# A streaming logsumexp: heads shared anew between GpSimd and VectorE, summed one tile later, in stages

## The chip, the cores and the metric

The kernel runs on one core of one Trainium2 chip. The metric is device time in microseconds (us) of one execution. Engines: PE or TensorE multiplies matrices, DVE is VectorE, ACT is ScalarE, POOL is GpSimd, SP is SyncE, which here only issues transfers.

## The reference

For each of 8 batches, 2048 rows and 8 heads of 256 columns, add the head's bias, take the logsumexp over the 256 columns, and write each result twice in a row:

```
x_heads = x.reshape(B, S, H, Dh).transpose(0, 2, 1, 3) + bias[None, :, None, :]
x_tiled = np.repeat(x_heads, 2, axis=2)
mx = x_tiled.max(axis=-1, keepdims=True)
lse = mx.squeeze(-1) + np.log(np.exp(x_tiled - mx).sum(axis=-1))
```

The input is 134 MB of float32, the output 1 MB. The kernel leaves out the maximum: it sums exp(x + b), or exp(x) times exp(b), and takes the logarithm.

## The kernel before

The rows are cut into T = 64 tiles of 256 rows (8 a batch); a tile is 128 partitions x K = 2 rows x 2048 columns, 2 MB. Nine buffers `xts` hold tiles. The order on every engine is the order in the code (a manual schedule). SP issues the loads (L95): nine at the start, and at the end of step t the load of tile t - 1 + 9 (L322), once the buffer's last reader is done. The last two tiles are loaded in pieces (`LAST_CUTS`, L26): tile 62 in two halves (one row of each partition), tile 63 in two and five pieces.

Each tile's eight heads take one of three ways, all with exp on ScalarE:

- Heads 0 and 1: TensorE adds the bias into PSUM (`add_bias`, L154 and L159: a small matmul with the bias, split into three bf16 parts, then the tile through the identity). ScalarE takes exp of each head and sums it in the same instruction (`sum_biased`, L165), four instructions a tile.
- Heads 2 to 4: GpSimd adds the bias in place (`g_add`, L182, b_rep is the bias spread over the partitions). One step later ScalarE takes exp of all six (three heads, two rows, `exp_inplace`, L194) and VectorE sums them in one reduce (`g_sum`, L186).
- Heads 5 to 7: ScalarE takes exp of x alone (L194), and VectorE multiplies each head and row by exp(bias) and sums it in one instruction (`weigh`, L200), six a tile. exp(bias) lies in PSUM, in w_rep.

So a step t issues on ScalarE: exp of heads 5 to 7 of tile t, exp of heads 2 to 4 of tile t - 1, four sums of tile t; on VectorE: six weighs of tile t, one reduce of tile t - 1. The last two tiles have no GpSimd part (NLATE): ScalarE takes exp of heads 2 to 7 piece by piece, VectorE weighs all six.

The sums of a batch go to R. Two steps after a batch ends, `finish` (L211) transposes R on TensorE (L216), takes Ln on ScalarE (L229), and issues the store (L250), on SP in the bulk. At the end tile 62 has its own sums Ry, tile 63 Rz; their stores are on SP, and eight stores of the last batch's other tiles on GpSimd's queue.

Of the kernel before, what the change touches and what calls it, by code (L numbers as in the profile page):

```python
# [9 lines left out]
F32 = mybir.dt.float32  # L10
BF16 = mybir.dt.bfloat16
ACT = mybir.ActivationFunctionType
ALU = mybir.AluOpType


K = 2

NPE = 2
NG = 3
NLATE = 2
NBUF = 9

LAST_CUTS = [[0, 1024, 2048], [0, 512, 1024, 1536, 1792, 2048]]  # L26


@with_exitstack
def kernel(  # L30
# [6 lines left out]
    nc = tc.nc  # L37
    P = nc.NUM_PARTITIONS
    B, S, D = x.shape
    H, Dh = bias.shape  # L40
    assert D == H * Dh and S % (P * K) == 0
    NBLK = S // (P * K)
    T = B * NBLK
    CPE = NPE * Dh
    CW = D - CPE
    MM = 512
    assert CPE <= MM

    sb = ctx.enter_context(tc.tile_pool(name="sb", bufs=1))
    pp = ctx.enter_context(  # L50
        tc.tile_pool(name="pp", bufs=1, space=bass.MemoryType.PSUM)
    )

    brow = sb.tile([1, D], F32, name="brow")
    b_rep = sb.tile([P, NG * Dh], F32, name="b_rep")
    ident = sb.tile([P, P], F32, name="ident")
    ones = sb.tile([1, P], F32, name="ones")
    ones3 = sb.tile([3, P], BF16, name="ones3")
    b3 = sb.tile([3, CPE], BF16, name="b3")
    bparts = sb.tile([1, 3, CPE], BF16, name="bparts")  # L60
    brest = sb.tile([1, 2, CPE], F32, name="brest")

    nblk = [NBLK] * (B - 1) + [NBLK - 2]
    R = [sb.tile([P, K, H, nblk[b]], F32, name=f"R{b}") for b in range(B)]
    Ry = sb.tile([P, K, H], F32, name="Ry")
    Rz = sb.tile([P, K, H], F32, name="Rz")
    junk = [sb.tile([P, Dh], F32, name=f"junk{i}") for i in range(2)]
    res = [sb.tile([H * NBLK, P, K, 2], F32, name=f"res{i}") for i in range(2)]
    xts = [sb.tile([P, K, D], F32, name=f"xt{i}") for i in range(NBUF)]
    w_rep = pp.tile([P, CW], F32, name="w_rep")  # L70
    ps = [pp.tile([P, MM], F32, name=f"ps{i}") for i in range(4)]
    tpair = pp.tile([P, 2, K, P], F32, name="tpair")
    tps = [tpair[:, i] for i in range(2)]

    def pieces(t):

        left = T - 1 - t
        if left > 1:
            return [(0, K, 0, D)]
        cuts = [[0, D]] * K if left else LAST_CUTS  # L80
        return [
            (k, k + 1, c0, c1) for k in range(K) for c0, c1 in zip(cuts[k], cuts[k][1:])
        ]

    def rows_of(t):

        b, blk = divmod(t, NBLK)
        v = x[b, blk * P * K : (blk + 1) * P * K, :]
        if t < T - 1:
            return v.rearrange("(p k) d -> p k d", k=K)  # L90
        return v.rearrange("(k p) d -> p k d", k=K)

    def load(t):
        for k0, k1, c0, c1 in pieces(t):
            nc.sync.dma_start(  # L95
                out=xts[t % NBUF][:, k0:k1, c0:c1], in_=rows_of(t)[:, k0:k1, c0:c1]
            )
# [5 lines left out]
    for set_idx, (_name, funcs) in enumerate(get_activation_tables(nc.m.arch).items()):  # L103
        if ACT.Exp in funcs and ACT.Ln in funcs:
            nc.scalar.add_instruction(  # L105
                mybir.InstLoadActFuncSet(
                    name=nc.get_next_instruction_name(),
# [4 lines left out]
    nc.scalar.dma_start(out=brow, in_=bias.rearrange("h j -> (h j)").unsqueeze(0))  # L112
    for t in range(NBUF):
        load(t)
# [4 lines left out]

    bp = brow[:, 0:CPE]  # L120
    nc.gpsimd.tensor_copy(bparts[:, 0], bp)
# [5 lines left out]
        nc.gpsimd.dma_start(out=b3[i : i + 1, :], in_=bparts[:, i])  # L127

    for c in range(0, CW, MM):
        nc.tensor.matmul(  # L132
            w_rep[:, c : c + MM],
            lhsT=ones,
            rhs=brow[:, CPE + c : CPE + c + MM],
            start=True,
            stop=True,
        )
    nc.scalar.activation(out=b_rep, in_=w_rep[:, 0 : NG * Dh], func=ACT.Copy)  # L139
    for c in range(0, CW, MM):  # L140
        w = w_rep[:, c : c + MM]
        nc.scalar.activation(out=w, in_=w, func=ACT.Exp)  # L142


    n_ps = [0]
    n_junk = [0]

    def add_bias(views):

        got = []  # L150
        for v in views:
            p = ps[n_ps[0] % len(ps)]
            n_ps[0] += 1
            nc.tensor.matmul(  # L154
                p[:, 0:CPE], lhsT=ones3, rhs=b3, start=True, stop=False
            )
            got.append(p)
        for p, v in zip(got, views):
            nc.tensor.matmul(p[:, 0:CPE], lhsT=ident, rhs=v, start=False, stop=True)  # L159
        return got  # L160

    def sum_biased(p, dst):
        for h in range(NPE):
            c = h * Dh
            nc.scalar.activation(  # L165
                out=p[:, c : c + Dh],
                in_=p[:, c : c + Dh],
                func=ACT.Exp,
                accum_out=dst(h),
            )  # L170

    b_tile = bass.AP(
        tensor=b_rep.tensor,
        offset=b_rep.offset,
        ap=[b_rep.ap[0], [0, K], [1, NG * Dh]],
    )

    def g_part(t):
        return xts[t % NBUF][:, :, CPE : CPE + NG * Dh]

    def g_add(t):
        nc.gpsimd.tensor_tensor(out=g_part(t), in0=g_part(t), in1=b_tile, op=ALU.add)  # L182

    def g_sum(t):
        b, blk = divmod(t, NBLK)
        nc.vector.tensor_reduce(  # L186
            out=R[b][:, :, NPE : NPE + NG, blk],
            in_=g_part(t).rearrange("p k (h j) -> p k h j", j=Dh),
            op=ALU.add,
            axis=mybir.AxisListType.X,  # L190
        )

    def exp_inplace(v):
        nc.scalar.activation(out=v, in_=v, func=ACT.Exp)  # L194

    def weigh(v, h, dst):
        c = h * Dh - CPE
        j = junk[n_junk[0] % 2]
        n_junk[0] += 1
        nc.vector.tensor_tensor_reduce(  # L200
            out=j,
            in0=v,
            in1=w_rep[:, c : c + Dh],
            scale=1.0,
            scalar=0.0,
            op0=ALU.mult,
            op1=ALU.add,
            accum_out=dst,
        )
# [45 lines left out]
    def finish_batch(b, engine):  # L255
# [7 lines left out]
            engine,  # L263
        )

    for t in range(T):
        b, blk = divmod(t, NBLK)
        xt = xts[t % NBUF]
        left = T - 1 - t

        def sum_at(k, h):
            if left > 1:
                return R[b][:, k, h, blk : blk + 1]
            return (Ry if left else Rz)[:, k, h : h + 1]

        if left >= NLATE:

            got = add_bias([xt[:, k, 0:CPE] for k in range(K)])
            g_add(t)
            w0 = CPE + NG * Dh  # L280
            exp_inplace(xt[:, :, w0:D])
            if t:
                exp_inplace(g_part(t - 1))
            for k in range(K):
                sum_biased(got[k], lambda h: sum_at(k, h))
            for k in range(K):
                for c in range(w0, D, Dh):
                    weigh(xt[:, k, c : c + Dh], c // Dh, sum_at(k, c // Dh))
            if t:
                g_sum(t - 1)  # L290
        for k0, k1, c0, c1 in pieces(t) if left < NLATE else []:
            if left == 0 and c1 == D and k0 > 0:

                finish(
                    B - 1,
                    lambda k: Rz[:, k0 - 1],
                    1,
                    1,
                    S - (K - k0 + 1) * P,
                    0,  # L300
                    nc.sync,
                )
            if c0 == 0:
                got = add_bias([xt[:, k, 0:CPE] for k in range(k0, k1)])
            w0 = max(c0, CPE)
            if w0 < c1:
                exp_inplace(xt[:, k0:k1, w0:c1])
            if c0 == 0:
                for k in range(k0, k1):
                    sum_biased(got[k - k0], lambda h: sum_at(k, h))  # L310
            for k in range(k0, k1):
                for c in range(w0, c1, Dh):
                    weigh(xt[:, k, c : c + Dh], c // Dh, sum_at(k, c // Dh))
            if left == 0 and c0 == 0:
                if k0 == 0:
                    finish_batch(B - 1, nc.gpsimd)
                elif k0 == 1:
                    finish(B - 1, lambda k: Ry[:, k], 1, K, S - 2 * K * P, 0, nc.sync)
        if left == NLATE:
            exp_inplace(g_part(t))  # L320
            g_sum(t)
        if 0 < t and t - 1 + NBUF < T:  # L322
            load(t - 1 + NBUF)

        fb, at = divmod(t - 2, NBLK)
        if fb >= 0 and at == NBLK - 1:
            finish_batch(fb, nc.sync)
# [33 lines left out]
```

The softmax here doesn't subtract the row's maximum and nothing guards it: scores larger than these inputs give would overflow.

## Time and profile before

| what | value |
|---|---|
| median of 9 runs | 337.96 us (337.76 to 338.32) |
| the profiled execution's own time | 338.13 us |
| its span, first to last instruction | 336.4 us |
| busy: ScalarE, VectorE, TensorE, GpSimd | 301.4, 244.7, 233.8, 224.3 us |
| mean granted TensorE clock | 0.787 |
| transfers | 135.46 MB, mean 403 GB/s |
| instructions | 2806 |

How to read it: in the profile a group of instructions is one line: code line, engine, operation, output <- input, shapes, count, then busy time, mean ns of one, and the idle time of the engine just before them with what ended it. The slices cut the span into 40 equal parts of 8.41 us: a digit is the busy share in tenths. A line of the time-ordered list has start and length in us; two of a kind in a row can be one line. In the tables of stretches the columns are the stretch, its length, busy time of PE, PE's weight load, DVE, ACT and POOL (with the number of instructions), the granted TensorE clock, the share of the 16 DMA engines that is busy, and GB/s. In the last microseconds SP's last store runs; no other engine does.

### The profile page before, as it was taken

The numbers are of one execution on the slowest core, as the hardware profiler recorded it, in microseconds if no ns is written. First come the engines' busy times: TensorE is split into PE (matmuls) and PEld (weight loads), VectorE is DVE, ScalarE is ACT, GpSimd is POOL, SyncE is SP. The second block draws the span as 40 slices with busy tenths as digits, with TensorE's granted clock in tenths as the row PEclk, the third lists the DMA queues.
The fourth block names the chain that finished last, engine by engine and source line by source line (L and its number), as shares of the span: only waits on it lengthen the run. The fifth ranks groups of instructions, "written<-read, shape, count | busy, mean of one in ns | idle before, by whom it ended". The sixth has DMA issues, their size and how long they took to land.

```text
span 336.4 us, 2806 instructions
## 1 busy us (share of the span) xinstructions
PE 233.8 (70%) x410; PEld 68.7 (20%) x410; DVE 244.7 (73%) x856; ACT 301.4 (90%) x660; POOL 224.3 (67%) x84
## 2 busy tenths in 40 slices
PE   6297687756779477766676786595675866883961
PEld 2122222121122122221121121121121221121210
DVE  0248888798878768777868777777877777877784
ACT  1489999999999989999989999899998999998995
POOL 7866766766766766776666776666775776675704
PEclk9997877789765976789877758767877589578596
DMA  8999999999999999999999999999999999999910
GB/s 299 431 431 433 423 431 425 431 427 426 429 428 427 429 430 427 431 422 430 430 424 429 429 425 433 427 427 431 429 430 425 428 429 427 429 429 420 352 41 16
DMA packets 11204, 135.46 MB, mean 403 GB/s; under 512 B 1577, under 2 KB 1849, under 8 KB 2993
## 3 DMA queue, kind: packets, MB, share of 16 engines
q1 hardware_dynamic: 10832, 135.17, 95.1%
q0 software_dynamic: 352, 0.10, 0.2%
q14 instruction: 15, 0.12, 0.1%
q8 instruction: 3, 0.05, 0.1%
q10 hardware_dynamic: 2, 0.01, 0.0%
HBM read 134.23 MB, written 1.05 MB: 402 GB/s over the span
## 4 chain that ended last, share of the span: by engine, by line
DMA 71%; DVE 6%; ACT 5%; issue 1%; PE 0%; SPq 0%; ACTq 0%; DVEq 0%
DMA xt<-in_x_dram 71%; ACT xt L194 4%; DVE junk L200 3%; DVE R L186 2%; ACT ps L165 1%; ACT res L229 0%; PE ps L159 0%; PE tpair L216 0%; DVE Rz L200 0%; DVE R L200 0%; SPq L95 0%; ACTq L194 0%; DVEq L356 0%
## 5 line engine op out<-in xcount | busy, mean ns | idle before, releaser
L182 POOL TENSOR_TENSOR xt<-xt,b_rep 128x1536 f32<-128x1536 f32 x62 | 214.0, 3451 | 96.2 <-DMA xt<-in_x_dram 91.9
L159 PE MATMUL ps<-xt,ident 128*128 128x512 f32 x256 | 180.6, 843 | 76.0 <-DMA xt<-in_x_dram 75.4
L200 DVE CUSTOM_DVE_ANT_0 junk<-xt,w_rep 128x256 f32<-128x256 f32 x396 | 140.5, 418 | 86.6 <-ACT xt L194 86.6
L194 ACT ACTIVATE xt<-xt 128x1536 f32<-128x1536 f32 (+1 forms) x132 | 183.4, 1436 | 14.0 <-DMA xt<-in_x_dram 13.2
L186 DVE TENSOR_REDUCE R<-xt 128x6 f32<-128x1536 f32 x62 | 108.5, 1750 | 0.8 <-ACT xt L194 0.8
L165 ACT ACTIVATE ps<-ps 128x256 f32<-128x256 f32 x256 | 94.5, 369 | 10.1 <-PE ps L159 5.9
L159 PEld LDWEIGHTS ps<-xt,ident 128*128 128x128 f32 x256 | 56.7, 245 | 165.0 <-DMA xt<-in_x_dram 114.6
L154 PE MATMUL ps<-b,ones 3*128 3x512 bf16 x128 | 48.7, 453 | 13.5 <-ACT ps L165 7.2
L165 ACT ACTIVATION_READ_ACCUMULATOR ps<-ps 128x1 f32 x256 | 48.5, 190 | 0.0
L200 DVE DVE_READ_ACCUMULATOR2_ANT R<- 128x1 f32 x372 | 30.8, 83 | 0.0
L154 PEld LDWEIGHTS <-ones 3*128 3x128 bf16 x128 | 7.8, 96 | 77.7 <-issue 70.0
L250 POOL DMA_DIRECT2D out_dram<-res x8 | 4.0, 505 | 9.3 <-ACT res L229 9.3
L132 PE MATMUL w_rep<-brow,ones 1*128 1x512 f32 x6 | 5.5, 1078 | 2.8 <-DMA brow<-in_bias_dram 2.8
L229 ACT ACTIVATE res<-tpair 64x512 f32<-64x512 f32 (+3 forms) x11 | 5.9, 539 | 1.2 <-PE tpair L216 0.9
L139 ACT ACTIVATE b_rep<-w_rep 128x768 f32<-128x768 f32 x1 | 0.8, 811 | 6.3 <-PE w_rep L132 6.3
L216 PE MATMUL tpair<-ident,R 128*64 128x128 f32 (+1 forms) x16 | 4.1, 349 | 0.2 <-DVE R L186 0.2
L216 PEld LDWEIGHTS tpair<-ident,R 128*64 128x64 f32 (+1 forms) x16 | 2.1, 142 | 8.3 <-issue 4.3
L216 PE MATMUL tpair<-ident,Rz 128*8 128x128 f32 x2 | 0.7, 374 | 4.3 <-DVE Rz L200 4.3
L132 PEld LDWEIGHTS w_rep<-brow,ones 1*128 1x128 f32 x6 | 1.8, 323 | 4.9 <-issue 4.9
L216 PE MATMUL tpair<-ident,Ry 128*8 128x128 f32 x2 | 0.4, 273 | 2.9 <-ACT res L229 2.9
L105 ACT ACT_TABLE_LOAD x1 | 1.3, 1283 | 0.7 <-PEq L345 0.7
L142 ACT ACTIVATE w_rep<-w_rep 128x512 f32<-128x512 f32 x3 | 1.7, 582 | 0.1
(18 smaller groups left out, 9.2 us busy)
## 6 DMA issues: line engine op xcount, KB each, us to landing
xt<-in_x_dram SPq DMA_DIRECT2D x62, 2048.0 KB, 34.4
xt<-in_x_dram SPq DMA_DIRECT2D x2, 1024.0 KB, 31.6
xt<-in_x_dram SPq DMA_DIRECT2D x2, 512.0 KB
out_dram<-res SPq DMA_DIRECT2D x7, 128.0 KB, 34.6
xt<-in_x_dram SPq DMA_DIRECT2D x3, 256.0 KB, 16.9
xt<-in_x_dram SPq DMA_DIRECT2D x2, 128.0 KB, 8.6
out_dram<-res POOLq DMA_DIRECT2D x8, 12.0 KB, 1.7
b<-bparts POOLq DMA_DIRECT2D x3, 1.0 KB, 5.7
```

What stands on the lines that cost most here:

```text
L132: nc.tensor.matmul(w_rep[:, c : c + MM], lhsT=ones, rhs=brow[:, CPE + c : CPE + c + MM], start=True, stop=True,)
L142: nc.scalar.activation(out=w, in_=w, func=ACT.Exp)
L154: nc.tensor.matmul(p[:, 0:CPE], lhsT=ones3, rhs=b3, start=True, stop=False)
L159: nc.tensor.matmul(p[:, 0:CPE], lhsT=ident, rhs=v, start=False, stop=True)
L165: nc.scalar.activation(out=p[:, c : c + Dh], in_=p[:, c : c + Dh], func=ACT.Exp, accum_out=dst(h),)
L182: nc.gpsimd.tensor_tensor(out=g_part(t), in0=g_part(t), in1=b_tile, op=ALU.add)
L186: nc.vector.tensor_reduce(out=R[b][:, :, NPE : NPE + NG, blk], in_=g_part(t).rearrange("p k (h j) -> p k h j", j=Dh), op=ALU.add, axis=myb ...
L194: nc.scalar.activation(out=v, in_=v, func=ACT.Exp)
L200: nc.vector.tensor_tensor_reduce(out=j, in0=v, in1=w_rep[:, c : c + Dh], scale=1.0, scalar=0.0, op0=ALU.mult, op1=ALU.add, accum_out=dst,)
L216: nc.tensor.transpose(out=tps[i][0:nr, k], in_=src(k), identity=ident)
L229: nc.scalar.activation(out=rv, in_=tv, func=ACT.Ln)
L250: engine.dma_start(out=ov, in_=iv)
```

## The change

Tiles now belong to four stages. `pe` is the number of heads on TensorE, `g0` the first of the heads whose bias GpSimd adds, the heads between are multiplied by exp(bias) on VectorE.

- Tiles 0 to 48: TensorE heads 0 and 1, VectorE 2 and 3, GpSimd 4 to 7. With `late`, nothing of heads 2 to 7 is done in the tile's own step but GpSimd's add. One step later ScalarE takes exp of all six heads in one instruction, VectorE multiplies heads 2 and 3 (both rows) by exp(bias) in one instruction, in place, and sums all six heads in one reduce.
- Tiles 49 to 56: TensorE head 0, VectorE 1 to 4 by weighs in the tile's own step, GpSimd 5 to 7, their exp and reduce one step later.
- Tiles 57 to 60: the same, loaded and worked on in halves, "later" meaning one half later.
- Tiles 61 to 63: TensorE heads 0 and 1, VectorE weighs 2 to 7, no GpSimd part, in halves. Tile 63's second half is cut in 1024, 512 and 512 columns.

exp(bias) of heads 1 to 4 lies in PSUM (w_ps), of heads 5 to 7 in SBUF (w_sb). There are five PSUM buffers `ps` instead of four. The next load of a buffer is issued after the later part of its tile. On VectorE the changed kernel has 382 instructions in program order (waits that stand alone not counted) where the one before has 858; on TensorE both have about 400 before each fp32 matmul is split in two.

```diff
-NPE = 2
-NG = 3
-NLATE = 2
-LAST_CUTS = [[0, 1024, 2048], [0, 512, 1024, 1536, 1792, 2048]]
+BULK = dict(pe=2, g0=4, late=True)
+MIXED = dict(pe=1, g0=5, late=False)
+PROMPT = dict(pe=2, g0=8, late=False)
+STAGES = [(0, BULK, False), (49, MIXED, False), (57, MIXED, True), (61, PROMPT, True)]
+LAST_CUTS = [[0, 2048], [0, 1024, 1536, 2048]]
...
-    w_rep = pp.tile([P, CW], F32, name="w_rep")
-    ps = [pp.tile([P, MM], F32, name=f"ps{i}") for i in range(4)]
+    w_ps = pp.tile([P, W1 - W0], F32, name="w_ps")
+    ps = [pp.tile([P, MM], F32, name=f"ps{i}") for i in range(5)]
...
+    for i, c in enumerate(range(G0, D, MM)):
+        spread(ps[i], c, c + MM)
+        nc.scalar.activation(
+            out=b_rep[:, c - G0 : c - G0 + MM], in_=ps[i], func=ACT.Copy
+        )
+    for c in range(W0, W1, MM):
+        w = w_ps[:, c - W0 : c - W0 + MM]
+        spread(w, c, c + MM)
         nc.scalar.activation(out=w, in_=w, func=ACT.Exp)
+    nc.scalar.activation(out=w_sb, in_=b_rep[:, W1 - G0 :], func=ACT.Exp)
...
+    def g_add(m, xt, k0, k1):
+        c = m["g0"] * Dh
+        v = xt[:, k0:k1, c:D]
+        nc.gpsimd.tensor_tensor(
+            out=v, in0=v, in1=each_row(b_rep, c - G0, D - c, k1 - k0), op=ALU.add
+        )
...
+    def later(m, xt, k0, k1, sums):
+        h0 = m["pe"] if m["late"] else m["g0"]
+        v = xt[:, k0:k1, h0 * Dh : D]
+        exp_inplace(v)
+        if m["late"]:
+            n = (m["g0"] - h0) * Dh
+            f = v[:, :, 0:n]
+            nc.vector.tensor_tensor(
+                out=f, in0=f, in1=each_row(w_ps, h0 * Dh - W0, n, k1 - k0), op=ALU.mult,
+            )
         nc.vector.tensor_reduce(
+            out=sums[:, k0:k1, h0:H],
+            in_=v.rearrange("p k (h j) -> p k h j", j=Dh),
...
+    waiting = None
     for t in range(T):
...
+        for k0, k1, c0, c1 in pieces(t):
...
             if c0 == 0:
+                got = add_bias(m, [xt[:, k, 0 : m["pe"] * Dh] for k in range(k0, k1)])
+                if with_pool:
+                    g_add(m, xt, k0, k1)
+            if waiting:
+                waiting()
+            h0 = max(c0 // Dh, m["pe"])
+            h1 = min(c1 // Dh, m["g0"])
+            if h0 < h1 and not m["late"]:
+                exp_inplace(xt[:, k0:k1, h0 * Dh : h1 * Dh])
             if c0 == 0:
                 for k in range(k0, k1):
+                    sum_biased(m, got[k - k0], lambda h: sums[:, k, h : h + 1])
+            if not m["late"]:
+                for k in range(k0, k1):
+                    for h in range(h0, h1):
+                        weigh(
+                            xt[:, k, h * Dh : (h + 1) * Dh], h, sums[:, k, h : h + 1]
+                        )
+            def next_waiting(t=t, m=m, xt=xt, k0=k0, k1=k1, sums=sums):
+                if m["g0"] < H:
+                    later(m, xt, k0, k1, sums)
+                if k1 == K and t + NBUF < T:
+                    load(t + NBUF)
+            waiting = next_waiting
```

## The prediction

> **What bounds the kernel now.** I read first the slices and queues of the profile page (is it the transfers?), then the groups of instructions, then a table of the end in steps of 1 us, then the time-ordered list of the end. The slices:
>
> ```profile
> PEclk9997877789765976789877758767877589578596
> DMA  8999999999999999999999999999999999999910
> GB/s 299 431 431 433 423 431 425 431 427 426 429 428 427 429 430 427 431 422 430 430 424 429 429 425 433 427 427 431 429 430 425 428 429 427 429 429 420 352 41 16
> ...
> q1 hardware_dynamic: 10832, 135.17, 95.1%
> ...
> q14 instruction: 15, 0.12, 0.1%
> q8 instruction: 3, 0.05, 0.1%
> ```
>
> From slice 2 to slice 37 the transfers run at about 428 GB/s without a gap: in the bulk the input stream is the limit. Counting landings of the fastest of the 16 DMA engines (each load leaves 16 completion records), tiles 2 to 61 took 290.5 us, 4.92 us a tile. The other engines all fit into that:
>
> ```profile
> L182 POOL TENSOR_TENSOR xt<-xt,b_rep 128x1536 f32<-128x1536 f32 x62 | 214.0, 3451 | 96.2 <-DMA xt<-in_x_dram 91.9
> ...
> L200 DVE CUSTOM_DVE_ANT_0 junk<-xt,w_rep 128x256 f32<-128x256 f32 x396 | 140.5, 418 | 86.6 <-ACT xt L194 86.6
> L194 ACT ACTIVATE xt<-xt 128x1536 f32<-128x1536 f32 (+1 forms) x132 | 183.4, 1436 | 14.0 <-DMA xt<-in_x_dram 13.2
> L186 DVE TENSOR_REDUCE R<-xt 128x6 f32<-128x1536 f32 x62 | 108.5, 1750 | 0.8 <-ACT xt L194 0.8
> L165 ACT ACTIVATE ps<-ps 128x256 f32<-128x256 f32 x256 | 94.5, 369 | 10.1 <-PE ps L159 5.9
> ```
>
> GpSimd idles 92 us for data, ScalarE only 13: ScalarE is nearly as full as the transfers. So time can be won only behind the stream, in the last two slices. The table of the end (busy time, then clock, DMA share, GB/s):
>
> ```profile
> 317.00:318.00 1.00, 1.00 (x2) 0.34 (x1) 1.00 (x7) 1.00 (x1) 1.00 (x1) 0.50 0.86 318
> 318.00:319.00 1.00, 1.00 (x2) 0.00 (x0) 1.00 (x7) 0.97 (x5) 0.84 (x1) 0.50 0.49 174
> ...
> 323.00:324.00 1.00, 1.00 (x5) 0.26 (x4) 1.00 (x6) 0.97 (x5) 0.00 (x0) 1.00 0.06 25
> 324.00:325.00 1.00, 1.00 (x3) 0.25 (x2) 1.00 (x7) 1.00 (x1) 0.00 (x0) 1.00 0.07 25
> ```
>
> 25 GB/s with a share of 0.06 is one DMA engine of sixteen, still working when the others are done. The completion records say the same: of tile 61's load the first engine lands at 308.12, the second slowest some 4.0 us later, the slowest at 315.25. The first half of tile 62 is complete at 317.74, the last piece of tile 63 at 325.24. ScalarE is late even for that:
>
> ```profile
> 315.33 2.86 ACT L194 ACTIVATE xt<-xt 128x1536 f32<-128x1536 f32 x2 [0.21 <-DMA xt<-in_x_dram]
> ...
> 319.99 2.85 ACT L194 ACTIVATE xt<-xt 128x1536 f32<-128x1536 f32 x2
> ...
> 332.08 0.40 ACT L194 ACTIVATE xt<-xt 128x256 f32<-128x256 f32 x1
> ```
>
> Tile 61 holds ScalarE from 315.33 to 319.99 (two exps, four sums), so tile 62's half, there at 317.74, waits 2.25 us. From 319.99 ScalarE has no gap over 0.3 us until 332.48; then weigh, transpose and Ln to 333.78, and 2.62 us for the last store: span 336.4.
>
> **The bulk, tiles 0 to 48.** Per tile, against 4.92 us:
> - GpSimd adds 2048 elements a row, not 1536. 3.45 us x 2048/1536 = 4.60; the step from the 512-wide subtraction (1.14) gives 4.61. It idles 1.4 us a tile now, 0.3 after. Here a rule speaks against the change: the Trainium skill ("GPSIMD Engine Reference", section "Engine selection") gives elementwise work to VectorE because GpSimd is about twice as slow with two inputs. By that rule the extra head belongs on VectorE; but there it would cost two weighs, 0.68 us, of an engine that fills up too, while here it fits in idle time. The row decides: no cost as long as the add stays under 4.92.
> - ScalarE: two exps of 1536 occupy it 2.76 (163.56 to 166.32 in the list); one of 3072 saves one start, about 0.1, so 2.66. Four sums stay at 1.88. 4.54, formerly 4.64.
> - VectorE loses six weighs (0.342 apart) and the reduce (1.68): 3.8 with waits. It gains a multiply of 1024 and a reduce of 3072. No row shows a multiply alone: from the weigh, which also reads one operand from PSUM, it lies between 4 x 0.27 = 1.07 (the weigh without its fixed part, about 0.07) and 4 x 0.342 = 1.37; I take 1.2. The reduce: 2 x 1.68 = 3.36, or 3.28 with one start saved. Sum 4.5, at most 4.75 with the wait between the two. Under 4.92.
> - TensorE is unchanged: 3.78 + 1.0 us a tile where the clock is 0.50, 2.6 where it is 1.
> - New waits: the joint exp waits for GpSimd's add of its tile. In ScalarE's queue the sums of the next tile stand behind it. The add ends 4.65 after landing, before the next tile lands; those sums wait for TensorE anyway. The multiply and reduce of a tile end about 4.65 + 2.7 + 4.5 = 11.9 us after landing, now about 11.2; then SP issues the load nine tiles on. That load has 34.4 us from issue to landing today, seven tiles deep; a microsecond less of queue starves nothing. Cost 0; if VectorE or GpSimd exceeded 4.92 it would be 49 times the excess.
> - Set-up: b_rep needs two spread matmul pairs instead of three, but in two copies; GpSimd is busy until 8.7 either way and starts near 9. One more exp (w_sb, about 0.8) fits before 17.5, where ScalarE waits for TensorE. 0.
>
> **Tiles 49 to 60.** GpSimd back at 3.45 (1.73 a half), VectorE eight weighs and a reduce, 8 x 0.342 + 1.68 = 4.4; ScalarE 1.8 + 1.38 + 2 x 0.47 + starts, 4.3; TensorE half its columns. Everything is faster than the stream, so ScalarE arrives at tile 61 with nothing left over. The loads in halves issue more often on SP, but each needs only the landing of the eighth before it. 0.
>
> **Tiles 61 to 63.** No GpSimd part, nothing late: a half is one exp (1.38) and two sums (0.89), 2.26 as in 323.63 to 325.89. A half lands every 2.46 (317.74 to 320.20). So ScalarE starts a half as it lands, save that TensorE at clock 0.5 needs 1.9 for it: the sums then start 0.5 late, once. VectorE needs 6 x 0.342 = 2.05. The 2.25 us of lateness go away, and the last tile has four pieces instead of seven: one exp less. **First gain, near 3 us.**
>
> **What the fewer instructions do.** The slowest engine's lag over the fastest grows in steps of about 1 us: 2.4 near 118 us, then 3.35, 4.35, 5.29, 6.14, 7.06 at the landings of 128.9, 169.4, 214.7, 260.1, 310.3: every 45 us. The two instruction queues carried 0.17 MB for 2806 instructions, 61 bytes each; a packet of 8 KB (0.12 MB in 15) holds some 130. VectorE runs 14 a tile with waits (six weighs, six accumulator reads, reduce, one wait): 130/14 x 4.92 = 46 us. So I read the lag as VectorE's instruction fetches, served by one DMA engine (inference, not shown directly). The change cuts VectorE's stream from 858 instructions to 382, waits not counted. Bounds: it saves nothing if the lag has another cause; at most half of 7 us. The second slowest engine lags 4.0 and keeps doing so, because TensorE's and most of ScalarE's streams are as long as before. I take a lag of 4.0. **Second gain: the last landings come 3.0 us earlier.**
>
> **The sum.** Landings: first half of 62 at 317.74 - 3.0 = 314.7. ScalarE 315.3 with TensorE's 0.5; three halves x 2.26 to 322.1; Ln 0.48; piece of 1024 with its sums 1.42; Ln 0.48; exp 0.53; Ln 0.40; exp 0.53: 325.9. Two weighs 0.9, transpose to Ln 0.84 (332.95 to 333.78), store 2.62: 330.3. With 0.5 for waits between pieces, 330.8. The profiled run took 338.13 for a span of 336.4, 1.73 more; it lay 0.17 over the median. 330.8 + 1.73 - 0.17 = **332.4**.
>
> **Rivals.**
> 1. *The lag stays* (0.22). Then the halves land as now and only the first gain counts: 330.8 + 3.0 = 333.8 span, 335.4. For it: no view shows whose instructions a packet carries. Against: the 45 us period fits VectorE's alone.
> 2. *The gain is eaten at the end* (0.07). The lag stays and ScalarE still enters tile 61 about 2.25 late, through GpSimd's last adds or TensorE at half clock: 337.7. Against: 0.6 us of slack a tile over twelve tiles.
> 3. *Slower: VectorE's multiply shuts out GpSimd* (0.15). The Trainium skill ("SBUF — State Buffer", section "Who interferes with whom") says that a VectorE instruction with two SBUF inputs and a GpSimd instruction that reads SBUF block each other outright. The multiply takes its factors from w_ps in PSUM, and beside today's weighs, which do the same, the add took 3.45 us, 3.42 while VectorE was idle at 9.20: by the row nothing is added. By the rule applied in full, 4.6 + 1.2 = 5.8 a tile, 0.9 over the stream, 43 us after 49 tiles, of which ScalarE can win back some 6 later: about 369. It decides from 5.1 us per add. VectorE over 5.05 a tile would end likewise, cheaper.
>
> **How the numbers follow.** Likeliest 0.56, its own range 331 to 334. A measurement tells 0.2% from no change. Faster are the first case and rival 1, 0.78; within 0.2% rival 2, 0.07; slower 0.15. Rival 3 is left out of the range, which runs from 330.0 (lag near 2.5, or full TensorE clock and no waits between pieces) to 336.8 (rival 1 with part of rival 2).
>
> **What would show it.** GpSimd's add near 4.6 us and idle about 0.3; VectorE multiply near 1.2, reduce near 3.3; GB/s as before to slice 37; the slowest completion of a late load about 4 us after the first, not 7; ScalarE idle, waiting for transfers, in tiles 57 to 62; the last exp ending 4 to 5 us before the end. An add over 5.1, or a VectorE without idle time in the bulk, would make me wrong on the slow side.

## The result and the profile after

| | before | changed | predicted |
|---|---|---|---|
| median | 338.04 us (337.65 to 338.41, 31 runs) | 333.72 us (333.47 to 335.23, 10 runs) | 332.4 us |
| ratio to before, 95% | 1 | 0.9884 [0.9875, 0.9893] | 0.983 |
| the profiled execution's own time | 338.13 us | 334.69 us | |
| its span | 336.4 us | 332.9 us | 330.8 us |
| instructions | 2806 | 2370 | |
| mean granted TensorE clock | 0.787 | 0.736 | |

The change saves 4.3 us by the medians, 3.9 by the ratio, which is that of the means (334.1 to 338.0 us); 5.6 were forecast. The changed kernel's executions lie in two bands, most near 333.6 and three near 335.2. The profiled one, at 334.69, is thus 1.0 above the median; what sets the band is not settled.

The slices and queues of the changed kernel's page:

```profile
PEclk9998969577895789865877789587876555555656
DMA  8999999999999999999999999999999999999930
GB/s 300 426 437 429 423 432 419 435 431 419 426 433 432 419 437 426 427 422 439 412 435 427 433 419 437 425 428 425 437 425 426 427 433 418 416 424 421 420 150 17
...
q14 instruction: 12, 0.10, 0.1%
q8 instruction: 3, 0.05, 0.1%
```

The stream runs at the same rate as before; that it fills slice 38 too is owed mostly to the shorter slices (8.32 us for 8.41). There are three fewer packets of instructions, 12 for 15. The TensorE clock falls to 5 or 6 tenths from slice 32 on, at 258 us, where the mixed stage gives TensorE one head instead of two.

Next, the groups of the bulk with different shapes kept apart (instructions | busy us, mean ns | idle before them and what ended it):

```profile
L195 POOL TENSOR_TENSOR xt<-xt,b_rep 128x2048 f32<-128x2048 f32 x49 | 222.2, 4535 | 20.1 <-DMA xt<-in_x_dram 17.9 <-ACT ps L177 1.0 <-DVE xt L210 0.8
L216 DVE TENSOR_REDUCE R<-xt 128x12 f32<-128x3072 f32 x49 | 164.4, 3355 | 5.8 <-DVE xt L210 1.0
L200 ACT ACTIVATE xt<-xt 128x3072 f32<-128x3072 f32 x49 | 135.1, 2758 | 7.5 <-POOL xt L195 7.4
L210 DVE TENSOR_TENSOR xt<-xt,w_ps 128x1024 f32<-128x1024 f32 x49 | 59.6, 1216 | 30.4 <-ACT xt L200 30.4
```

GpSimd's add takes 4.54 us and then waits 0.4 us a tile for data: the bulk is still the stream's. VectorE needs 1.22 + 3.36 = 4.57 us a tile.

The table of the end (stretch, length, busy time of PE, weight load, DVE, ACT, POOL, then clock, DMA share, GB/s):

```profile
318.00:319.00 1.00, 1.00 (x2) 0.00 (x0) 0.91 (x6) 0.99 (x1) 0.00 (x0) 0.50 0.82 299
...
322.00:323.00 1.00, 1.00 (x4) 0.26 (x2) 1.00 (x7) 0.66 (x3) 0.00 (x0) 0.50 0.04 16
323.00:324.00 1.00, 1.00 (x2) 0.50 (x2) 1.00 (x8) 1.00 (x4) 0.00 (x0) 0.50 0.00 0
```

At 323 the loads are over, where before one engine of sixteen went on past 325. But ScalarE is idle for a third of 322 to 323, and the clock is 0.50 where it was 1.00. The time-ordered list of ScalarE says why it matters (start, length, then the idle time before and its releaser):

```profile
315.25 1.47 ACT L200 ACTIVATE xt<-xt 128x1536 f32<-128x1536 f32 x1
...
320.39 1.48 ACT L200 ACTIVATE xt<-xt 128x1536 f32<-128x1536 f32 x1
322.31 0.37 ACT L177 ACTIVATE ps<-ps 128x256 f32<-128x256 f32 x1 [0.44 <-PE ps L171]
...
324.75 0.37 ACT L177 ACTIVATE ps<-ps 128x256 f32<-128x256 f32 x1 [0.47 <-PE ps L171]
...
327.81 0.37 ACT L257 ACTIVATE res<-tpair 8x256 f32<-8x256 f32 x1 [1.08 <-DMA out_dram<-res]
328.09 0.61 ACT L200 ACTIVATE xt<-xt 128x512 f32<-128x512 f32 x1
330.07 0.37 ACT L257 ACTIVATE res<-tpair 8x256 f32<-8x256 f32 x1 [1.37 <-PE tpair L244]
```

Tile 62's first half is complete at 314.86 and its exp starts at 315.25: the lateness of 2.25 us is gone. Three new gaps stand behind it. Two are sums that wait for TensorE (0.44 and 0.47; the last gap, 1.37, is the weighs, transpose and their start, which the prediction counted). The third is the Ln of tile 63's first row, which waits 1.08 us for a store to finish reading the `res` buffer that it writes. The last exp, whose data landed at 322.70, is queued behind that Ln and starts at 328.09.

For the experiments one table is kept, of profiled executions. "Lag" is how long the slowest of the 16 DMA engines completes after the fastest, over the loads of tiles 61 and 62. "Behind" is the time from the last load's completion to the end of the last Ln.

| kernel | VectorE instructions with waits | lag | last load complete | last Ln ends | behind |
|---|---|---|---|---|---|
| before | 932 | 7.1 | 325.24 | 333.78 | 8.54 |
| changed | 508 | 4.0 | 322.70 | 330.44 | 7.74 |
| e1, memsets on VectorE | 1304 | 10.2 | 328.31 | 336.71 | 8.40 |
| e2, memsets on GpSimd | 932 | 7.3 | 325.30 | 333.64 | 8.34 |
| e3, bulk alone | 312 | 3.9 | 322.09 | 333.53 | 11.44 |
| e4, end alone | 998 | 7.2 | 325.58 | 332.75 | 7.17 |
| e8, end in another order | 508 | 3.7 | 322.37 | 328.72 | 6.35 |
| e10, bulk to tile 56 | 396 | 3.8 | 322.10 | 330.47 | 8.37 |
| e11, bulk to tile 60 | 332 | 3.6 | 321.98 | 332.78 | 10.80 |

Below some 500 VectorE instructions the lag falls no further than 3.6. Five kernels of 508 to 512 VectorE instructions (the changed one, e6 to e9) lie between 3.5 and 4.3, so differences of this size among the short streams say nothing. The two parts of the gain are read from the table: the last load is complete 2.54 us earlier, and the work behind it is 0.80 us shorter.

### The profile page after: what moved, and what is told of

Its sections match the earlier page's. It is cut to its first block, busy times and chain, and to the rows that moved or that the text cites. A ratio compares the mean times of both kernels' runs of the same rounds, so it can differ in the third digit from the quotient of the medians.

```text
span 332.9 us, 2370 instructions
## 1 busy us (share of the span) xinstructions
PE 227.3 (68%) x412; PEld 72.3 (22%) x412; DVE 288.2 (87%) x380; ACT 291.6 (88%) x570; POOL 274.6 (82%) x87
## 4 chain that ended last, share of the span: by engine, by line
DMA 55%; ACT 14%; POOL 8%; issue 8%; PE 7%; DVE 7%; POOLq 0%; DVEq 0%; SPq 0%; ACTq 0%
DMA xt<-in_x_dram 51%; ACT xt L200 10%; POOL xt L195 7%; PE ps L171 5%; ACT ps L177 4%; DVE xt L210 3%; DVE R L216 3%; DMA b<-bparts 2%; PE ps L166 1%; DMA brow<-in_bias_dram 1%; PE tpair L244 1%; DMA out_dram<-res 0%; POOL brest L133 0%; POOL brest L131 0%; ACT res L257 0%
## 5 line engine op out<-in xcount | busy, mean ns | idle before, releaser
L195 POOL TENSOR_TENSOR xt<-xt,b_rep 128x2048 f32<-128x2048 f32 (+2 forms) x65 | 264.2, 4067 | 35.5 <-DMA xt<-in_x_dram 28.7
L171 PE MATMUL ps<-xt,ident 128*128 128x512 f32 (+1 forms) x256 | 173.5, 814 | 73.0 <-DMA xt<-in_x_dram 72.7
L200 ACT ACTIVATE xt<-xt 128x3072 f32<-128x3072 f32 (+3 forms) x89 | 184.8, 2094 | 12.4 <-POOL xt L195 12.1
L216 DVE TENSOR_REDUCE R<-xt 128x12 f32<-128x3072 f32 (+2 forms) x65 | 186.2, 2864 | 5.8 <-DVE xt L210 1.0
L177 ACT ACTIVATE ps<-ps 128x256 f32<-128x256 f32 x232 | 85.6, 369 | 15.0 <-PE ps L171 11.0
L210 DVE TENSOR_TENSOR xt<-xt,w_ps 128x1024 f32<-128x1024 f32 x49 | 59.6, 1216 | 30.4 <-ACT xt L200 30.4
L166 PE MATMUL ps<-b,ones 3*128 3x512 bf16 (+1 forms) x128 | 47.8, 444 | 10.3 <-ACT ps L177 6.1
L228 DVE CUSTOM_DVE_ANT_0 junk<-xt,w_ps 128x256 f32<-128x256 f32 x114 | 40.8, 424 | 3.1 <-ACT xt L200 2.8
L228 DVE DVE_READ_ACCUMULATOR2_ANT R<- 128x1 f32 x108 | 10.0, 92 | 0.0
L228 DVE CUSTOM_DVE_ANT_0 junk<-xt,w_sb 128x256 f32<-128x256 f32 x18 | 6.8, 423 | 1.2 <-ACT xt L200 1.2
```

The lines of the kernel that those rows point to most:

```text
L166: nc.tensor.matmul(p[:, 0:n], lhsT=ones3, rhs=b3[:, 0:n], start=True, stop=False)
L171: nc.tensor.matmul(p[:, 0:n], lhsT=ident, rhs=v, start=False, stop=True)
L177: nc.scalar.activation(out=p[:, c : c + Dh], in_=p[:, c : c + Dh], func=ACT.Exp, accum_out=dst(h),)
L195: nc.gpsimd.tensor_tensor(out=v, in0=v, in1=each_row(b_rep, c - G0, D - c, k1 - k0), op=ALU.add)
L210: nc.vector.tensor_tensor(out=f, in0=f, in1=each_row(w_ps, h0 * Dh - W0, n, k1 - k0), op=ALU.mult,)
L216: nc.vector.tensor_reduce(out=sums[:, k0:k1, h0:H], in_=v.rearrange("p k (h j) -> p k h j", j=Dh), op=ALU.add, axis=mybir.AxisListType.X,)
```

## Experiments

### Whose instructions delay the loads: e1 and e2

The step of the prediction that was only inferred is that VectorE's instruction fetches hold up one DMA engine. Both kernels are the kernel before with 372 idle instructions added, on one engine or the other. Each instruction writes a single zero to a buffer that nothing reads.

```diff
+    pads = [sb.tile([1, 1], F32, name=f"pad{i}") for i in range(6)]
...
+            for pad in pads:
+                nc.vector.memset(pad, 0.0)      # e1, after g_sum
+                nc.gpsimd.memset(pad, 0.0)      # e2 instead, after g_add
```

> The kernel before, with six one-element memsets on VectorE after each reduce of tiles 0 to 61: 372 more instructions that no other engine waits for, and work that fits in VectorE's idle time of 1.1 us a tile. Theory (the slowest DMA engine is the one that fetches VectorE's instructions): 20 instructions a tile instead of 14, a step of about 1 us every 32 us instead of every 45, so the slowest completion of a late load lags the fastest by about 10 us, not 7.1. ScalarE was 2.25 us late for the landings in the kernel before, so only what exceeds that shows at the end: 0.6 to 1.2 us slower. Rival (the lag has another cause, such as the transfers themselves): lag 7.1, time within 0.3 us of the kernel before.

> The kernel before, with the same six memsets a tile on GpSimd after its add (about 0.6 us of its 1.4 us idle time). Theory: the 372 instructions are fetched by another DMA engine than VectorE's, whose lag grows by some 3 us but stays under 7, so the slowest lag stays 7.1 and the time within 0.3 us. Rival (any instruction delays the slowest engine, whoever runs it): lag near 10 and 0.6 to 1.2 us slower, as with VectorE.

Measured: e1 341.09 us, 1.009 [1.0076, 1.0105], so 3.1 us slower. e2 338.01 us, 0.9998 [0.999, 1.0007]: nothing. Lines of e1's page and of its table of stretches, which answer to those shown of before:

```profile
L293 DVE MEMSET pad<- 1x1 f32 x372 | 8.2, 59 | 0.0
```

```profile
326.00:327.00 1.00, 0.81 (x5) 0.33 (x4) 1.00 (x6) 0.97 (x5) 0.00 (x0) 1.00 0.07 27
327.00:328.00 1.00, 1.00 (x2) 0.19 (x2) 1.00 (x7) 1.00 (x2) 0.00 (x0) 1.00 0.06 23
```

The memsets keep VectorE busy for 8.2 us in all, 0.13 us a tile, on an engine that idled 1.4 us a tile before its weighs (86.6 us in 62 tiles) and still does (85.1). What they move is the lone DMA engine: at 327 it still runs at 23 GB/s with a share of 0.06, three microseconds later than before. Both kernels have three more packets of instructions (18 for 15), but only VectorE's move the lag: 7.1 to 10.2 in e1, 7.3 in e2. That shows it for VectorE's instruction stream, and the size fits: 1.0 us of lag for each 8-KB packet, some 124 instructions.

The kept traces also have the time of each packet, which the prediction didn't use. In the kernel before, the last four steps of the slowest engine's lag come with the load that lands after a packet at 167.89, 212.46 (another follows at 213.18), 258.63 and 308.23 us; in e1 the last five come after packets at 186.01, 219.70, 250.64, 285.58 and 316.81. So the lag grows at the fetches, 45 to 50 us apart before and 31 to 35 in e1, and not with VectorE's work. In e2 the added packets lie some 80 us apart (122.14, 202.91, 283.67) and, to judge by the order of the lags, push another DMA engine: after the last of them the third slowest lags 3.46 us instead of 2.79, while the slowest lags 6.35. GpSimd's fetches aren't free; the engine that carries them had room.

The size that e1 was expected to lose was too small, and this matters. ScalarE's 2.25 us of lateness at tile 62 were taken for a backlog that would swallow part of a later landing. ScalarE's list of e1, tiles 61 and 62:

```profile
318.38 2.86 ACT L195 ACTIVATE xt<-xt 128x1536 f32<-128x1536 f32 x2 [1.25 <-DMA xt<-in_x_dram]
...
322.93 2.85 ACT L195 ACTIVATE xt<-xt 128x1536 f32<-128x1536 f32 x2
```

Tile 62's half lands at 320.71 and its exp starts at 322.93, late by 2.22 again, though ScalarE had waited 1.25 us for tile 61. The lateness is not a backlog but an order: two exps and four sums of tile 61 start when tile 61 lands and stand in front. It moves with the landing: the last load is complete 3.07 us later than before, and the time is 3.07 us longer.

### Each half of the change alone: e3 and e4

Both kernels are the changed one with other stages. e3 has the bulk's division up to tile 61 and the last two tiles as before. e4 has the old division up to tile 48 and the changed one from there.

```diff
-STAGES = [(0, BULK, False), (49, MIXED, False), (57, MIXED, True), (61, PROMPT, True)]
+STAGES = [(0, BULK, False), (62, PROMPT, True)]          # e3, with the old LAST_CUTS
...
+OLD = dict(pe=2, g0=5, late=False)                       # e4
+STAGES = [(0, OLD, False), (49, MIXED, False), (57, MIXED, True), (61, PROMPT, True)]
```

> The changed kernel with its bulk form kept up to tile 61 and with the last two tiles cut and treated as in the kernel before (no stages 49 to 60, tile 63 in two and five pieces). Theory: VectorE's stream is shorter still, the slowest lag 3.5 to 4.2 us, so the last load lands 2.5 to 3 us sooner than in the kernel before; but ScalarE comes to tile 62 with tile 61's later part still to do (2.7 us) and the end has one piece more: 1 to 3 us faster than before, slower than the changed kernel by 1 to 3. Rival (all of the gain is in the stages of the end): as the kernel before, 338.

> The changed kernel with tiles 0 to 48 as in the kernel before: TensorE two heads, three weighed, three added by GpSimd; the stages from tile 49 on as changed. Theory: VectorE runs as many instructions as before, and 7 us of lag come back; the stages let ScalarE start each half as it lands, so about 2.5 us slower than the changed kernel and 1.5 to 2.5 faster than before, 336. Rival (the lag doesn't matter): as the changed kernel, 333.7.

Measured: e3 338.22 us, 1.0008 [1.0, 1.0017]: no gain at all. e4 336.99 us, 0.9974 [0.9964, 0.9984]: 1.0 us faster. The sum of the two, 0.8, is a fifth of what both give together, and both gave less than was expected of them. ScalarE's list of e3 says where the earlier landing went:

```profile
316.71 4.14 ACT L200 ACTIVATE xt<-xt 128x3072 f32<-128x3072 f32 x2 [0.36 <-POOL xt L195]
...
327.51 0.37 ACT L177 ACTIVATE ps<-ps 128x256 f32<-128x256 f32 x1 [0.67 <-PE ps L171]
...
331.55 0.37 ACT L257 ACTIVATE res<-tpair 8x256 f32<-8x256 f32 x1 [0.84 <-DMA out_dram<-res]
```

The last load is complete at 322.09, 3.15 us earlier than before. But tile 61 belongs to the bulk here: its six heads pass GpSimd first (4.5 us), and their exp of 3072 starts only at 316.71, in front of tile 62's half, which landed at 314.46. The two together run to 320.85. The work behind the last load grows from 8.54 to 11.44 us. Its two later waits, 0.67 for TensorE and 0.84 for a store, are of the kind seen in the changed kernel. In e4 it shrinks to 7.17, but the lag stays at 7.2 and the last load is even 0.34 later. Two things keep e4's gain small: tile 62's first half lands at 318.11 and its exp still starts 0.61 late, at 318.72, and the Ln of tile 63's first row waits for a store as in the changed kernel:

```profile
330.12 0.37 ACT L258 ACTIVATE res<-tpair 8x256 f32<-8x256 f32 x1 [1.08 <-DMA out_dram<-res]
```

What an earlier landing is worth by itself e3 doesn't say, because it brings a new order with it; the bulk's form up to tile 48 with the old division behind it was not run. With the new stages in place the bulk is worth 3.0 us by the ratios and 3.3 by the medians (e4 against the changed kernel, whose last load is complete 2.88 us earlier), and in e1 a later landing cost its full length. So in both cases the landing counted nearly in full; in e3 something new stood in front of the last pieces, which is what the stages prevent.

### How long the bulk may last: e10 and e11

```diff
-STAGES = [(0, BULK, False), (49, MIXED, False), (57, MIXED, True), (61, PROMPT, True)]
+STAGES = [(0, BULK, False), (57, MIXED, True), (61, PROMPT, True)]      # e10
+STAGES = [(0, BULK, False), (61, PROMPT, True)]                         # e11
```

> The changed kernel with the bulk's form up to tile 56 (no stage 49 to 56). Theory: the bulk runs at the pace of the stream with idle time on GpSimd, VectorE and ScalarE from about 150 us on, so it leaves nothing to catch up and the stage 49 to 56 brings nothing; VectorE's stream is some 120 instructions shorter, the lag 3.5 to 4.2: within 0.5 us of the changed kernel, 333.2 to 334.2. Rival: the bulk hands over late work, and 1 to 2 us are lost, 335.

> The changed kernel with the bulk's form up to tile 60, then halves with no GpSimd part (61 to 63) as changed. Theory: what counts at the end is that ScalarE starts tile 61's halves as they land; here tile 60's joint exp (2.66) and multiply and reduce (4.57) stand in front of them, half of it made up over three tiles that have 0.2 us of slack a half: 1 to 2 us slower than the changed kernel, 335. Rival: only the last two tiles matter, 333.7.

Measured: e10 334.84 us (334.71 to 335.48), 0.9906 [0.9893, 0.992]; e11 336.78 us, 0.9959 [0.9946, 0.9971]. So with no mixed stage at all 3.1 us of the 4.3 are lost by the medians (2.5 of 3.9 by the ratios), with only its tiles 49 to 56 taken out 1.1 (0.75 by the ratios). A line of e11's list:

```profile
311.77 4.12 ACT L200 ACTIVATE xt<-xt 128x3072 f32<-128x3072 f32 x2
```

It is e3's case one tile earlier: tile 60's joint exp stands in front of tile 61's half, and ScalarE does not catch up again (the last Ln ends 10.80 us behind the last load). That e11 lost more than expected has this reason.

e10 lost more than expected as well, though its interval touches that of the changed kernel (at 0.9893). Its trace shows what the stage of tiles 49 to 56 is for: VectorE. There VectorE goes over from the previous tile's work to its own tile's. In the changed kernel GpSimd's add of tile 49 starts at 252.16 and VectorE's first weigh of that tile at 259.24, 7.1 us later; VectorE then has no pause over 0.11 us until 314.50, when it has caught up, just ahead of tile 62. In e10 it has none from 295.82 to 328.77, and the Ln of tile 63's first row waits 1.14 us for a transpose that waits for VectorE's sums. That loss takes the place of the store's wait of 1.08, and the two profiled spans are equal, 332.9. Where the 1.1 us between the medians lie is not seen in them: e10's four executions (334.7 to 335.5) lie near the changed kernel's upper band, and why stays open.

### The shared port: e5

The rival on the slow side was that VectorE's multiply shuts out GpSimd. It was argued away by the place of the factors, PSUM. e5 copies the factors to SBUF and multiplies by the copy.

```diff
+    w_mul = sb.tile([P, 2 * Dh], F32, name="w_mul")
+    nc.scalar.activation(out=w_mul, in_=w_ps[:, Dh : 3 * Dh], func=ACT.Copy)
...
-                in1=each_row(w_ps, h0 * Dh - W0, n, k1 - k0),
+                in1=each_row(w_mul, 0, n, k1 - k0),
```

> The changed kernel with the factors exp(bias) of the bulk's multiply in SBUF instead of PSUM; nothing else differs. The rule of the shared port read in full: VectorE's multiply (1.22 us) and GpSimd's add (4.53) shut each other out, so a tile needs 5.75 us of the two where the stream gives 4.92; 49 tiles make some 40 us, of which little can be won back: about 365 to 372. Rival (the trace's only hint, adds that run at the same speed beside any VectorE work): 333.7 as before, multiply 1.22 and add 4.53.

Measured: 365.68 us (three executions at 365.7, a fourth at 373.11, which the ratio leaves out), 1.0819 [1.0803, 1.0836]. The groups of e5 by shape:

```profile
L197 POOL TENSOR_TENSOR xt<-xt,b_rep 128x2048 f32<-128x2048 f32 x49 | 264.8, 5439 | 1.4 <-DMA xt<-in_x_dram 1.4
...
L212 DVE TENSOR_TENSOR xt<-xt,w_mul 128x1024 f32<-128x1024 f32 x49 | 106.2, 2167 | 21.2 <-ACT xt L202 21.2
```

The add takes 5.44 us for 4.54, the multiply 2.17 for 1.22. GpSimd no longer waits for data, and VectorE waits once, at the start (21.2 us): both need about 5.5 us a tile (VectorE 2.17 + 3.35), over the stream's 4.92 by more than half a microsecond. This is the Trainium skill's rule ("SBUF — State Buffer", section "Who interferes with whom"), which bars the two engines from each other when VectorE takes both inputs from SBUF. It holds here, at 0.90 us a tile instead of the multiply's full 1.22. So the rival was no fiction: it is 32 us, of which GpSimd's 49 adds of the bulk with their waits make 24 (266.2 for 242.3 us), the rest not traced; a choice of memory for 2 KB a partition keeps it out.

### TensorE at half clock: e6

In the changed kernel TensorE is granted less in the mixed stage and 0.50 at the end. The Trainium skill ("TensorE: Matmul & The Clock Gate", section "What's actually happening") has the clock follow how busy TensorE was in the last few microseconds. e6 gives it more to do in tiles 49 to 60: head 0 goes through the identity a second time into columns that nobody reads.

```diff
+        twice = m["pe"] == 1
+        nb = 2 * n
...
+            if twice:
+                nc.tensor.matmul(p[:, n:nb], lhsT=ident, rhs=v, start=True, stop=True)
```

> The changed kernel; in tiles 49 to 60 TensorE also multiplies head 0 a second time into columns that nobody reads, so its work there is nearly that of the bulk. Theory: the granted clock was 0.50 in those tiles because TensorE had little to do; with more work it is granted about 0.75, and ScalarE's waits for TensorE in tiles 61 to 63 (0.57, 0.52, 0.44, 0.47 us) shrink: 0.5 to 1 us faster, 332.7 to 333.2. Rival: the clock of the end is set by the last tiles' own pauses, 333.7 as the changed kernel.

Measured: 335.03 us (333.58 to 335.10), 0.9905 [0.9889, 0.992]: no gain. Four of its five executions lie near 335.0, one at 333.6, the changed kernel's two bands again. The mixed stage by stretches, first of the changed kernel, then of e6:

```profile
290.00:309.00 19.00, 11.90 (x25) 4.65 (x24) 19.00 (x79) 18.19 (x33) 14.31 (x9) 0.50 1.01 423
```

```profile
290.00:309.00 19.00, 14.10 (x42) 8.03 (x41) 19.00 (x79) 17.80 (x33) 14.39 (x9) 0.77 1.01 421
```

In the mixed stage the trace agrees with the rule: with TensorE busy 63% of the stretch the clock stays at 0.50, with 74% (and at the faster clock) it is 0.77. The share alone doesn't decide: in the kernel before TensorE was busy 78% of the 6 us from 309 to 315 at a clock of 0.53. And in the last halves, where the two sums wait, the clock is 0.50 in e6 as well (0.50 in the stretches from 319 to 324), and the waits are 0.59 and 0.73. Warming the stage before does nothing for the end. What sets the end's clock stays open. Pauses alone don't explain it: from 318 to 324 the trace counts TensorE as busy for 5.82 of 6 us in the changed kernel and 5.35 in e6, and the clock is 0.50 in both. That doesn't fit the rule, unless these busy times, whose ends are modelled, are too long.

### The waits of the end: e7, e8 and e9

e7 gives each of the last Ln's its own `res` buffer, so that none waits for a store. e8 keeps that and changes the order of the end on ScalarE: tile 62's Ln ahead of the last half, the three exps of the last half ahead of its two sums and of the other Ln. e9 is e8 with no TensorE head in the last half, eight weighs on VectorE instead (exp(bias) of head 0 for it lies in SBUF).

```diff
-    res = [sb.tile([H * NBLK, P, K, 2], F32, name=f"res{i}") for i in range(2)]
+    res = [sb.tile([H * NBLK, P, K, 2], F32, name=f"res{i}") for i in range(4)]
...
-        rs = res[i]
+        rs = res[i if r is None else r]
...
+            last = t == T - 1 and k0 == K - 1                        # e8
+            if last and c0 == 0:
+                finish(B - 1, lambda k: Ry[:, k], 1, K, S - 2 * K * P, 0, nc.sync)
...
-            if c0 == 0:
+            if c1 == D if last else c0 == 0:
                 for k in range(k0, k1):
                     sum_biased(m, got[k - k0], lambda h: sums[:, k, h : h + 1])
...
+FINAL = dict(pe=0, g0=8, late=False)                                 # e9
+            m = FINAL if last else mode_of(t)
```

> The changed kernel with four output buffers res instead of two, so that the Ln of tile 63's first half doesn't wait 1.08 us for the store of tile 62 that reads the same buffer. Theory: that wait stands in front of the last exp, and all of it shows: 0.9 to 1.1 us faster, 332.7. Rival: the next wait (for TensorE, or for the landing) takes its place, 333.5.

> As e7, and in the last half ScalarE takes the exps of the three pieces before the two sums that wait for TensorE and before tile 63's first Ln; tile 62's Ln goes ahead of the half. Theory: the end was a chain of waits in ScalarE's fixed order; its last Ln then ends about 2.6 us sooner than in the changed kernel: 331.1. Rival: the end is bound by the last landing (322.7 in the changed kernel) and the work behind it, and only e7's 1 us is won: 332.7.

> As e8, and the very last half (second half of tile 63) leaves TensorE out: VectorE weighs all its eight heads. Theory: in e8 the end still waits for TensorE at half clock (landing at 319.8, then 2.09 for the half before, transposes, 2.02 for the last half, sums, 327.6); without it the end is VectorE's eight weighs, done near 326.9, and the last Ln near 327.8 instead of 328.7: 0.8 to 1 us faster than e8, 332.1, and less spread from run to run. Rival: VectorE's two more weighs or the eight stores on GpSimd's queue (landed at 329.3 in the changed kernel) take the place: 333, as e8.

Measured: e7 333.43 us (332.16 to 334.07), 0.986 [0.984, 0.988]; e8 333.0 us (332.25 to 333.45), 0.985 [0.9835, 0.9865]; e9 333.69 us, 0.9866 [0.9851, 0.9881]. All three are slower than was expected of them, and near what their rivals said. In e7 the store's wait is gone, but the wait of the last two sums for TensorE is 0.99 in its profile (of its slowest execution, 334.07), not 0.47. The median gains 0.3, the ratio 0.8; the intervals overlap, so this is not told from no gain. ScalarE's list of e8:

```profile
321.98 0.37 ACT L177 ACTIVATE ps<-ps 128x256 f32<-128x256 f32 x1 [0.59 <-PE ps L171]
...
324.11 0.59 ACT L257 ACTIVATE res<-tpair 8x512 f32<-8x512 f32 x1 [0.68 <-PE tpair L244]
324.61 1.65 ACT L200 ACTIVATE xt<-xt 128x512 f32<-128x512 f32 x3
326.65 0.37 ACT L177 ACTIVATE ps<-ps 128x256 f32<-128x256 f32 x1 [0.39 <-PE ps L171]
```

The exps now run in one piece at 324.61 and the last Ln ends at 328.72, 1.72 us before that of the changed kernel. e8 has the lowest median of all, and its interval ends at 0.9865, below the changed kernel's 0.9875: by the medians it is 0.7 us better, by the ratios 1.1. Its interval overlaps those of e7 and e9, so what the order adds to the buffers is not told apart. Of what was hoped for in the order, the Ln ahead of the exps took back 0.68: it waits for tile 62's transpose. e9 takes away the sums' wait, and loses it again: its eight weighs follow the exps one by one, from 325.97 to 328.8 on VectorE, and are what the last transpose and Ln wait for (2.12 us of idle time on ScalarE).

## Why the prediction was right, and where it was off

- **The stream bounds the bulk, and no engine exceeds it: right.** Add 4.54 us (4.60 said), multiply 1.22 (1.2), reduce 3.36 (3.28 to 3.36), joint exp 2.76 (2.66 from start to start). GpSimd waits 0.4 us a tile (0.3 said).
- **The skill's objection to GpSimd** was rightly set aside by the row: the fourth head fits into its idle time. **The shared port** was rightly kept out by the row of the weighs with PSUM operands, and e5 gives the rival's size, 365.7 us where 369 was worked out.
- **VectorE's fetches make the lag: right, and shown by e1 and e2.** The lag of 4.0 that the second slowest engine suggested came out at 4.0 for tile 62 (314.86 for its first half, 314.7 said). A packet at 318.10 then took the lag from 3.97 to 4.27, so tile 63's first row, complete at 320.15, landed 0.55 us later than said. The landings of the end came 2.5 to 2.9 us earlier than before instead of 3.0.
- **ScalarE starts a half as it lands: right** for tile 62 (315.25 and 317.52, said 315.3 and 317.6). Its slack before was smaller than the 0.6 us a tile said: in the stretch from 290 to 309, near the end of the mixed stage, it was busy 18.19 of 19 us, 0.2 idle a tile, because the exps of a tile in halves take 2 x 1.04 + 2 x 0.84 us instead of 1.89 + 1.48. It sufficed. VectorE's 4.4 us a tile was right (4.45 from weigh to weigh), but the prediction overlooked that VectorE enters tile 49 some 7 us behind; at half a microsecond won a tile, the twelve tiles were just enough, which was luck.
- **The term that was off most is the last of the sum, "With 0.5 for waits between pieces".** These waits measured 0.44 + 0.47 for TensorE (one more of 0.52, at 319.51, lay ahead of a landing and cost at most 0.24) and 1.08 for the store that reads `res`: 1.99 us, 1.5 over the allowance. With the 0.55 of tile 63's landing that is 2.0, about the 2.1 us by which the profiled span (332.9) exceeds the one said (330.8); by the median the miss is 1.3 us. The store's wait could have been seen from the code: two `res` buffers for the last four Ln's, and an exp in ScalarE's queue behind the second user of the first.
- **"First gain, near 3 us" was too large.** The end alone gave 1.0 us (e4, where rival 1's number for that case was 335.4 and the run 337.0), where 0.6 us of the lateness stayed and the store's wait of 1.08 stood too. The second gain came out at 3.0 to 3.3 us once the stages were there, near the 3.0 said. That the bulk alone gave nothing (e3) was not foreseen: the lateness of 2.25 us was read as something that ScalarE carries along; e1 showed that it is an order in the queue, and in e3 a new order, the joint exp of 3072 ahead of the half, cost all that the landing gave.

## What to carry to other kernels

When a kernel is bound by its stream, count an engine's instructions as traffic too: the loads are complete when the slowest DMA engine is, and here that is the one which VectorE's instructions share. An earlier landing is worth its length only if nothing new stands in fixed order ahead of the last pieces, so ask what does, on every engine that the end waits for, and which buffers the last results share. Where GpSimd adds through SBUF beside a VectorE multiply, as here, leave the multiply's second operand in PSUM.

## What the runs showed of the hardware

- 372 more VectorE instructions, three packets of 8 KB, cost 3.1 us of lag and 3.1 us of time; three more packets for GpSimd's cost no time: the slowest engine's lag stayed at 7.3, and another's grew. A packet itself takes 0.31 to 0.35 us in the trace of e1, and its step in the lag is 1.0; the rest is not explained.
- VectorE's multiply with both inputs in SBUF and GpSimd's add lengthen each other by 0.95 and 0.90 us, three quarters of the multiply's 1.22. So a part of the two seems to run side by side; no run shows a multiply from SBUF without an add beside it.
- TensorE's clock was 0.53 from 250 to 290 us and 0.50 from 290 to 309, where it had been 0.77 and 0.76 with twice the columns; more work there (e6) brought 0.75 and 0.77, but left 0.50 from 318 to 324.
- The changed kernel falls in two bands 1.6 us apart (333.6 and 335.2), and so does e6, with no cause that these runs isolate; the kernel before spreads over 0.8 us in 31 runs.
